# Moving k's transposes into the scores' bank, one factor from VectorE to GpSimd, and two PSUM pools swapped, in a hybrid attention and mLSTM decoder step

## The chip, the cores and the metric

The kernel runs on one core of one Trainium2 chip. The metric is device time in microseconds (us) of that core. PE is the matmul engine (TensorE), DVE is VectorE, ACT is ScalarE, POOL is GpSimd and SP is SyncE, which here only issues DMAs. Each engine takes its own instructions in a fixed order; semaphores hold one back until another engine has done its part.

## The reference, cut to what matters

One decoder layer for 1024 prompt tokens and 8 sample tokens. The change touches the chunkwise mLSTM, the attention of the samples and the gated feed-forward:

```python
h = rmsnorm(x, g_attn_norm); z = h @ w_in
q_a, k_a, v_a, q_m, k_m, v_m, o_m, i_pre, f_pre, gate_a, gate_m = jnp.split(z, in_split_points(), axis=-1)
...
def step(carry, inp):                       # mLSTM, one chunk of tokens
    c, n, m = carry
    ...
    w = d * jnp.einsum('bhtd,bhsd->bhts', qc, kc)
    num = inter[..., None] * jnp.einsum('bhvd,bhtd->bhtv', c, qc) + jnp.einsum('bhts,bhsv->bhtv', w, vc)
    ...
    w_s = jnp.exp(a + b[..., -1:] - m_end[..., None])
    c_new = decay[..., None, None] * c + jnp.einsum('bhs,bhsv,bhsd->bhvd', w_s, vc, kc)
...
x = x + mixed @ w_out
h2 = rmsnorm(x, g_ffn_norm)
x = x + (jax.nn.silu(h2 @ w_gate) * (h2 @ w_up)) @ w_down
```

## The kernel before, in words

All large products run on PE as three passes of split operands (`hh`, `hl` are the high and low parts of the normalised input, `wh`, `wl` those of a weight slice). The first half of the program walks over 128-wide slices of `w_in`: for each slice three column chunks of 344 are multiplied (`gemm`, L226) and evacuated. Between these matmuls a list of generators (`side`) is stepped at a fixed rate; so mLSTM and attention are laid in small pieces between the matmuls of the slices `k`, `v`, `q` and `o`.

The mLSTM works in 8 rounds of 128 tokens, numbered 0 to 7 here by their chunk `c`. `mlstm_a(c)` puts on PE: the scores of the four heads into two banks, `ms_0` and `ms_1` (L559, pool `pa`, each using only the first 256 of a bank's 512 columns); four transposes of v into `mvt` (L563, pool `pt`); two transposes of k into `mkt` (L567, pool `pt`). DVE then multiplies the decay matrix `bmb` by the scores, first those of `ms_0`, then those of `ms_1`, and multiplies the transposed k by a column of weights (`kq` from `mkt`). ACT copies `mvt` to `va`. `mlstm_b` of the round before follows on PE (`my`), then `mlstm_u` (`mu`, which reads `kq`) and `mlstm_d` (transposes into `mh`, pool `pt`, copied by ACT to `hm`). Pool `pt` has two banks, `pa` and `pg` three each; a tile of a pool must wait until the tile that had its bank before has been read.

`mlstm_sample` runs among the rounds; from round 4 to round 6 it gives DVE eight operations on 128x1024 elements (`st`, `scc`, `snum`). `attn_sample` runs among the steps of the prompt's attention. Each `yield` in such a generator ends one piece of it.

What sets the order: PE, SP and POOL keep the order in which the code is written, and so does what is issued through `main_line` on DVE and ACT. The rest of DVE and ACT is placed by a list scheduler, so an edit can reorder them.

After the first part come the gate products (`GateVisit`, tiles `ag`, `bg`, `cg`, `dg`) and, later, the feed-forward (`UpVisit`, `af`, `bf`, `cf`, `df`). Both use a pool `pd` of three tiles of two banks each, laid over the six banks that `pg` and `pa` had. A visit makes seven products, `SEQ`. The first feed-forward visit is split into two single-set visits, on 258 columns each; the other 21 take 516 columns. After the products of a visit, `after` issues the rest: `s1f` and `s2f` get a factor `R`, then a Silu on ACT (L1625), then `R` again (`scale` inside `gate`).

Of the kernel before, what the change touches and what calls it, by code (L numbers as in the profile page):

```python
# [15 lines left out]
ALU = mybir.AluOpType  # L16
# [68 lines left out]
def decoder_step(ctx, tc, x_prompt, x_sample, cache_k, cache_v, st_c, st_n, st_m, rel_bias, w_in, b_if, sinks,  # L85
# [13 lines left out]
    sq = ctx.enter_context(tc.tile_pool(name="sq", bufs=2))  # L99
    pt = ctx.enter_context(tc.tile_pool(name="pt", bufs=2, space=PSUM))  # L100
    banks = ExitStack()
    pg = banks.enter_context(tc.tile_pool(name="pg", bufs=3, space=PSUM))
    pa = banks.enter_context(tc.tile_pool(name="pa", bufs=3, space=PSUM))
    dp = ctx.enter_context(tc.tile_pool(name="dp", bufs=1, space=DRAM))

    def U(name, dt=F32, shape=None):
# [14 lines left out]
    def ps_t(name):  # L121
        return pt.tile([P, 512], F32, tag="t", name=name)
# [426 lines left out]
    def mlstm_a(c, st):  # L549
        bmb, kq, col = st  # L550
        t0 = slice(c * P, (c + 1) * P)
        va = T(f"va{c}", [P, 4, P + 1])
        dve.memset(va[:, :, P:P + 1], 1.0)
        bm2 = bmb.rearrange("p (j u) t -> p u j t", u=2)
        for u in range(2):
            o = 64 * u
            sps = ps_a(f"ms{c}_{u}")
            for j in range(2):
                pe.matmul(sps[:, j * P:(j + 1) * P], mk[j][o:o + 64, t0], mq[j][o:o + 64, t0], start=True, stop=True)  # L559
            tt(dve, bm2[:, u], bm2[:, u], sps[:, 0:256].rearrange("p (j t) -> p j t", t=P), ALU.mult)  # L560
        vps = ps_t(f"mvt{c}")
        for hd in range(4):
            pe.transpose(vps[:, hd * P:(hd + 1) * P], mv[hd][:, t0], ident)  # L563
        act.copy(va[:, :, 0:P], vps.rearrange("p (h v) -> p h v", v=P))
        kps = ps_t(f"mkt{c}")
        for j in range(2):
            pe.transpose(kps[:, j * P:(j + 1) * P], mk[j][:, t0], ident)  # L567
        kw = kq[:, 0:2, :].rearrange("p a (b d) -> p (a b) d", d=64)
        tt(dve, kw, kps[:, 0:256].rearrange("p (h d) -> p h d", d=64), col[:, 1, :].unsqueeze(2).to_broadcast([P, 4, 64]), ALU.mult)
        return bmb, va, kq, kw, col  # L570

    def mlstm_b(c, st):
# [354 lines left out]
    def attn_sample():  # L927
        sc = slice(NP, NT)
        ks = U("ks", shape=[P, NS, P])
        vs = U("vs", shape=[P, NS, P])  # L930
        sp.dma_start(ks, cache_k[0].rearrange("b j k d -> j b (k d)"))
        sp.dma_start(vs, cache_v[0].rearrange("b j k d -> j b (k d)"))
        ps = ps_t("snew")
        pe.transpose(ps[0:NS, 0:P], kT[:, sc], ident)
        pe.transpose(ps[0:NS, P:2 * P], vT[:, sc], ident)
        new = T("snewt", [NS, 2 * P])
        act.copy(new, ps[0:NS, 0:2 * P])
        pool.dma_start(ks[0:1, :, :], new[:, 0:P])
        pool.dma_start(vs[0:1, :, :], new[:, P:2 * P])
        for dst, src, o in ((s_kw, cache_k, 0), (s_vw, cache_v, P)):  # L940
            pool.dma_start(dst[0, :, 0:P - 1], src[0, :, 1:P])
            pool.dma_start(dst[0, :, P - 1].rearrange("b k d -> b (k d)"), new[:, o:o + P])
        for _ in range(AS[0]):
            yield
        kst = U("kst", shape=[P, NS, P])
        for g in range(2):
            ps = ps_t(f"kst{g}")
            for j in range(4):
                pe.transpose(ps[:, j * P:(j + 1) * P], ks[:, 4 * g + j, :], ident)
            act.copy(kst[:, 4 * g:4 * g + 4, :], ps.rearrange("p (b d) -> p b d", d=P))  # L950
        for _ in range(AS[1]):
            yield
        qb = S("qb", [P, NS, 8], 1)
        pool.memset(qb, 0.0)
        for i in range(4):
            pool.tensor_copy(qb[0:64, :, i], qT[i][0:64, sc])
            pool.tensor_copy(qb[64:128, :, 4 + i], qT[i][64:128, sc])
        for _ in range(AS[2]):
            yield
        ps = ps_t("ssT")  # L960
        for b in range(NS):
            pe.matmul(ps[:, 8 * b:8 * b + 8], kst[:, b, :], qb[:, b, :], start=True, stop=True)
        sT = S("sT", [P, 64], 1)
        act.copy(sT, ps[:, 0:64])
        for _ in range(AS[3]):
            yield
        ps = ps_t("ss")
        pe.transpose(ps[0:64, 0:P], sT, ident)
        pr = S("spr", [64, P], 1)
        c = S("sc4", [64, 4], 1)  # L970
        dve.tensor_tensor_reduce(out=pr, in0=ps[0:64, 0:P], in1=bias_s, scale=1.0, scalar=NEG, op0=ALU.add, op1=ALU.max,
                                 accum_out=c[:, 0:1])
        tt(dve, c[:, 0:1], c[:, 0:1], sinks_s, ALU.max)
        tt(dve, c[:, 2:3], sinks_s, c[:, 0:1], ALU.subtract)
        dve.tensor_scalar(c[:, 0:1], c[:, 0:1], -1.0, None, op0=ALU.mult)
        act.activation(pr, pr, AF.Exp, bias=c[:, 0:1], accum_out=c[:, 1:2])
        act.activation(c[:, 2:3], c[:, 2:3], AF.Exp)
        tt(dve, c[:, 1:2], c[:, 1:2], c[:, 2:3], ALU.add)
        dve.reciprocal(out=c[:, 1:2], in_=c[:, 1:2])
        dve.tensor_scalar(pr, pr, c[:, 1:2], None, op0=ALU.mult)  # L980
        for _ in range(AS[4]):
            yield
        ps = ps_t("spt")
        pe.transpose(ps[:, 0:64], pr, ident[0:64, 0:64])
        pT = S("spT", [P, 64], 1)
        act.copy(pT, ps[:, 0:64])
        for _ in range(AS[5]):
            yield
        ps = ps_t("spv")
        for b in range(NS):  # L990
            pe.matmul(ps[:, 8 * b:8 * b + 8], vs[:, b, :], pT[:, 8 * b:8 * b + 8], start=True, stop=True)
        pv = ps[:, 0:64].rearrange("p (b h) -> p h b", h=8)
        for i in range(4):
            dve.tensor_copy(yat[i][0:64, sc], pv[0:64, i, :])
            dve.tensor_copy(yat[i][64:128, sc], pv[64:128, 4 + i, :])
# [601 lines left out]
    class UpVisit(Visit):  # L1597
# [16 lines left out]
        def after(self, n, sets):  # L1614

            box, now, later = self.box, [], []
            s0, s1 = sets[0], sets[-1] + 1
            get = lambda b: self.view(box[b], sets)
            eng = dve if len(sets) == 1 else pool

            def scale(s, th):
                tt(eng, s, s, R["r"][:, th, s0:s1], ALU.mult)

            def gate(s, th):
                act.activation(s, s, AF.Silu)  # L1625
                scale(s, th)
            if n == 0:
                box["p1"] = self.small("p1", sets)
                now.append(lambda: act.copy(box["p1"], get("a")))
            elif n == 2:  # L1630
                box["s1"] = self.small("s1", sets)
                (later if sets == (0,) else now).extend([lambda: tt(dve, box["s1"], get("b"), box["p1"], ALU.add),
                                                         lambda: scale(box["s1"], 0)])
                later.append(lambda: gate(box["s1"], 0))
            elif n == 1:
                box["U2"] = self.small("U2", sets)
                now.append(lambda: act.copy(box["U2"], get("a")))
            elif n == 3:
                box["V"] = self.small("V", sets)
                now.append(lambda: act.copy(box["V"], get("a")))  # L1640

                def c22():
                    if "uu" not in box:
                        box["uu"] = U(f"uu{self.m}", shape=[P, 2, 2, HB])
                    tt(dve, box["uu"][:, 1, s0:s1], get("d"), box["V"], ALU.add)
                later.append(c22)
            elif n == 5:
                box["s2"] = self.small("s2", sets)
                if self.apart(sets):
                    now.append(lambda: tt(dve, box["s2"], get("c"), box["V"], ALU.add))  # L1650
                    now.append(lambda: scale(box["s2"], 1))
                else:
                    now.append(lambda: tt(dve, box["s2"], get("a"), R["r"][:, 1, s0:s1], ALU.mult))
                later.append(lambda: gate(box["s2"], 1))
            elif n == 6:
                u1 = box["uu"][:, 0, s0:s1]
                now.append(lambda: tt(dve, u1, get("d"), box["U2"], ALU.add))
                later.append(lambda: tt(dve, u1, u1, box["s1"], ALU.mult))
                later.append(lambda: tt(dve, box["uu"][:, 1, s0:s1], box["uu"][:, 1, s0:s1], box["s2"], ALU.mult))
            return now, later  # L1660
# [607 lines left out]
```

## Time and profile before

| | |
|---|---|
| time, median of 3 runs | 1391.66 us (1391.24 to 1391.66) |
| the profiled execution: its time, its span | 1391.65 us, 1389.9 us |
| PE busy | 1369.4 us (99%) |
| DVE, ACT, POOL busy | 975.4 us (70%), 617.0 us (44%), 242.0 us (17%) |
| mean granted TensorE clock | 0.997 |

The span is the time from the first to the last instruction in the trace; the 1.75 us beside it lie before and after. Matmuls overlap in the pipeline, so two of them that follow each other without a wait start 0.1 to 0.2 us apart though each is shown with 0.3 us. A square bracket at the end of a row of the timeline gives the idle time of that engine ahead of the row and what ended it.

### The profile page before, as it was taken

Reading aid. Unit: us, or ns where it says so; the run is one execution under the profiler, and the core shown is the slowest. Engines: PE = TensorE matmul, PEld = TensorE weight load, DVE = VectorE, ACT = ScalarE, POOL = GpSimd, SP = SyncE. Lnnn points to the kernel's source line nnn. Section 1 sums busy time; section 2 is a strip of 40 time slices with the busy share of each in tenths; the row PEclk is TensorE's granted clock in tenths of the full one; section 3 lists DMA queues with packets and bytes.
Section 4 is the critical chain, followed back from the end, with each engine's and each line's share of the span. In section 5 each row is a group of like instructions: output and inputs, shape, how many; then the busy total and the mean of one; then the engine's idle time right before and its main releaser. Section 6 shows DMA issues by size and latency. Waiting matters only on the chain.

```text
span 1389.9 us, 26966 instructions
## 1 busy us (share of the span) xinstructions
PE 1369.4 (99%) x10723; PEld 1337.9 (96%) x10724; DVE 975.4 (70%) x1853; ACT 617.0 (44%) x1407; POOL 242.0 (17%) x303
## 2 busy tenths in 40 slices
PE   9999999999999999999999999999999999999996
PEld 7999889999999999999999999999999999999996
DVE  7252758886944444755587888898888878888875
ACT  6243567654443331374454343444433343333325
POOL 4012111001111100001132232333333220000003
PEclk9999999999999999999999999999999999999998
DMA  7144224114233274788423344544434468677633
GB/s 224 32 117 113 62 63 100 31 62 149 81 107 100 84 283 137 221 281 283 166 77 120 110 153 153 168 168 139 131 114 144 146 214 304 220 239 237 221 123 122
DMA packets 179173, 208.42 MB, mean 150 GB/s; under 512 B 20638, under 2 KB 137634, under 8 KB 179032
## 3 DMA queue, kind: packets, MB, share of 16 engines
q1 hardware_dynamic: 161928, 151.72, 35.1%
q0 software_dynamic: 16688, 54.40, 10.7%
q8 instruction: 84, 1.38, 0.4%
q10 hardware_dynamic: 432, 0.59, 0.1%
q14 instruction: 41, 0.34, 0.1%
HBM read 140.31 MB, written 68.96 MB: 151 GB/s over the span
## 4 chain that ended last, share of the span: by engine, by line
PE 90%; DVE 3%; ACT 2%; DMA 2%; issue 1%; POOL 0%; SPq 0%; ACTq 0%; POOLq 0%; DVEq 0%
PE af L1589 18%; PE df L1589 9%; PE ad L1589 7%; PE wo L1261 6%; PE bf L1589 5%; PE ag L1589 4%; PE dd L1589 4%; PE o L226 3%; PE mv L226 3%; PE wm L1385 3%; PE wa L1385 3%; PE q L226 3%; PE dg L1589 2%; PE bd L1589 2%; PE mk L226 2%; PE gm L226 2%
## 5 line engine op out<-in xcount | busy, mean ns | idle before, releaser
L125 POOL TENSOR_TENSOR s1f<-s1f,R 128x516 f32<-128x516 f32 x42 | 68.8, 1637 | 87.2 <-DVE s1f L125 71.5
L1589 PE MATMUL df<-Th,op6f 128*128 128x258 f32 x352 | 67.3, 283 | 1.3 <-DVE uu L125 1.3
L1589 PE MATMUL af<-Th,op0f 128*128 128x258 f32 x352 | 67.4, 284 | 0.0
L1589 PE MATMUL bf<-Th,op2f 128*128 128x258 f32 x352 | 67.3, 283 | 0.0
L1589 PE MATMUL df<-Th,op4f 128*128 128x258 f32 x352 | 67.3, 284 | 0.0
L1589 PE MATMUL af<-Th,op1f 128*128 128x258 f32 x352 | 67.1, 283 | 0.0
L1589 PE MATMUL af<-Th,op3f 128*128 128x258 f32 x352 | 66.9, 283 | 0.0
L1589 PE MATMUL af<-Th,op5f 128*128 128x258 f32 x336 | 64.1, 283 | 0.0
L1625 ACT ACTIVATE s1f<-s1f 128x516 f32<-128x516 f32 (+1 forms) x23 | 14.2, 618 | 103.5 <-POOL s1f L125 103.5
L1589 PEld LDWEIGHTS df<-Th,op6f 128*128 128x128 f32 x352 | 55.9, 189 | 1.5 <-DVE uu L125 1.5
L1589 PEld LDWEIGHTS af<-Th,op1f 128*128 128x128 f32 x352 | 56.0, 189 | 0.0
L1589 PEld LDWEIGHTS af<-Th,op0f 128*128 128x128 f32 x352 | 56.0, 189 | 0.0
L1589 PEld LDWEIGHTS bf<-Th,op2f 128*128 128x128 f32 x352 | 56.0, 189 | 0.0
L1589 PEld LDWEIGHTS df<-Th,op4f 128*128 128x128 f32 x352 | 55.8, 189 | 0.0
L1589 PEld LDWEIGHTS af<-Th,op3f 128*128 128x128 f32 x352 | 55.6, 189 | 0.0
L1589 PEld LDWEIGHTS af<-Th,op5f 128*128 128x128 f32 x336 | 53.4, 190 | 0.0
L125 POOL TENSOR_TENSOR s2f<-s2f,R 128x516 f32<-128x516 f32 x21 | 27.4, 1307 | 135.5 <-ACT s2f L1625 135.4
L1589 PE MATMUL bf<-Tl,op2f 128*128 128x258 f32 x176 | 49.8, 283 | 0.0
L1589 PE MATMUL df<-Tl,op6f 128*128 128x258 f32 x176 | 49.7, 282 | 0.0
L1589 PE MATMUL af<-Tl,op1f 128*128 128x258 f32 x176 | 49.7, 282 | 0.0
L1589 PE MATMUL af<-Tl,op0f 128*128 128x258 f32 x176 | 49.7, 282 | 0.0
L1589 PE MATMUL df<-Tl,op4f 128*128 128x258 f32 x176 | 49.7, 282 | 0.0
(690 smaller groups left out, 4935.9 us busy)
## 6 DMA issues: line engine op xcount, KB each, us to landing
ta<-d_t SPq DMA_DIRECT2D x63, 516.0 KB, 6.6
Yd<-in_w_down_dram SPq DMA_DIRECT2D x40, 256.0 KB, 3.5
d_t<-h POOLq DMA_DIRECT2D x18, 516.0 KB, 5.2
d_t<-t POOLq DMA_DIRECT2D x18, 516.0 KB, 4.6
Xf<-in_w_gate_dram SPq DMA_DIRECT2D x22, 256.0 KB, 4.1
Xf<-in_w_up_dram SPq DMA_DIRECT2D x22, 256.0 KB, 6.9
Yf<-in_w_gate_dram SPq DMA_DIRECT2D x22, 256.0 KB, 3.0
Yf<-in_w_up_dram SPq DMA_DIRECT2D x22, 256.0 KB
```

The costliest lines, as they stand in the source:

```text
L125: return eng.tensor_tensor(out=out, in0=a, in1=b, op=op)
L226: pe.matmul(o, a[:, k, :], b[:, cs], start=(k == 0 and i == 0), stop=(k == n - 1 and i == len(passes) - 1))
L1261: pe.matmul(ps[:, th, 0:HB], a[:, k, :], b, start=(k == 0 and i == 0), stop=(k == KD - 1 and i == 2))
L1385: pe.matmul(ps[:, c, 0:CW], a[:, k, :], b[:, cs], start=(k == 0 and q == 0), stop=(k == 3 and q == 2))
L1589: pe.matmul(ps[:, s if ps.shape[1] > 1 else 0, 0:HB], a, b, start=(first and k == 0 and i == 0), stop=(k == self.nk - 1 and i == 2), skip_ ...
L1625: act.activation(s, s, AF.Silu)
```

## The change

Four edits. The k transposes go to columns 256 to 511 of the round's `ms_1`, in place of an own tile of `pt`. In the single-set visits the factor behind the Silu is issued on POOL in place of DVE; the factor ahead of the Silu stays where it was. `pa` is opened ahead of `pg`, so the two have each other's banks. The samples' attention gets one more `yield`, between its first and second group of key transposes, by which all its later pieces are one step later.

```diff
+    pa = banks.enter_context(tc.tile_pool(name="pa", bufs=3, space=PSUM))
     pg = banks.enter_context(tc.tile_pool(name="pg", bufs=3, space=PSUM))
-    pa = banks.enter_context(tc.tile_pool(name="pa", bufs=3, space=PSUM))
...
-        kps = ps_t(f"mkt{c}")
+        kps = sps[:, 256:512]
         for j in range(2):
             pe.transpose(kps[:, j * P:(j + 1) * P], mk[j][:, t0], ident)
...
-        tt(dve, kw, kps[:, 0:256].rearrange("p (h d) -> p h d", d=64), col[:, 1, :].unsqueeze(2).to_broadcast([P, 4, 64]), ALU.mult)
+        tt(dve, kw, kps.rearrange("p (h d) -> p h d", d=64), col[:, 1, :].unsqueeze(2).to_broadcast([P, 4, 64]), ALU.mult)
...
             act.copy(kst[:, 4 * g:4 * g + 4, :], ps.rearrange("p (b d) -> p b d", d=P))
+            if g == 0:
+                yield
...
-            def scale(s, th):
-                tt(eng, s, s, R["r"][:, th, s0:s1], ALU.mult)
+            def scale(s, th, on=None):
+                tt(on or eng, s, s, R["r"][:, th, s0:s1], ALU.mult)

             def gate(s, th):
                 act.activation(s, s, AF.Silu)
-                scale(s, th)
+                scale(s, th, pool)
```

On PE, in round 4 of the mLSTM, before: the last scores, the transposes of v (`mvt`) and of k (`mkt`), and the next matmuls of the slice `v`.

```order
L559 MATMUL ms_1_1730<-mq_139,mk_141 128x128
L563 MATMUL mvt_1734<-cst,mv_142 128x128
L563 MATMUL mvt_1734<-cst,mv_143 128x128
L563 MATMUL mvt_1734<-cst,mv_144 128x128
L563 MATMUL mvt_1734<-cst,mv_145 128x128
L567 MATMUL mkt_1740<-cst,mk_140 128x128 [waits Activation_49]
L567 MATMUL mkt_1740<-cst,mk_141 128x128
L226 MATMUL v_1720<-hh_124,wl_v 128x344
```

The same place on PE with the change.

```order
L559 MATMUL ms_1_1726<-mq_139,mk_141 128x128
L563 MATMUL mvt_1730<-cst,mv_142 128x128
L563 MATMUL mvt_1730<-cst,mv_143 128x128
L563 MATMUL mvt_1730<-cst,mv_144 128x128
L563 MATMUL mvt_1730<-cst,mv_145 128x128
L567 MATMUL ms_1_1726<-cst,mk_140 128x128 [waits DVE_49]
L567 MATMUL ms_1_1726<-cst,mk_141 128x128
L226 MATMUL v_1716<-hh_124,wl_v 128x344
```

The order of PE is the same. The k transposes wait for DVE where they waited for an ACT copy; the count that they wait for is the one that DVE gives when it has multiplied `bmb` by the same round's `ms_1`. It is so in all 8 rounds, while `mkt` before waited in rounds 1 to 3 for the `kq` multiply of the round before and in rounds 4 to 7 for ACT's copies of an earlier `mh`.

On DVE, in rounds 4 and 5, before: `st`, `scc` and `snum` are the wide steps of the samples' state, `wl_q` the low part of a weight slice, `num` the scaling of an earlier round's output.

```order
L619 TENSOR_SCALAR num_1632<-num_1632,mrd 128x128 x4
L125 TENSOR_TENSOR st_1416<-sv,sk 128x1024
L125 TENSOR_TENSOR bmb_1598<-bmb_1598,ms_0_1726 128x2x128
L125 TENSOR_TENSOR bmb_1598<-bmb_1598,ms_1_1730 128x2x128
...
L125 TENSOR_TENSOR st_1416<-scc_1415,sq 128x1024
L125 TENSOR_TENSOR bmb_1711<-bmb_1711,ms_0_1864 128x2x128
L125 TENSOR_TENSOR bmb_1711<-bmb_1711,ms_1_1868 128x2x128
L125 TENSOR_TENSOR mrd<-mrd,msq 128x4
L708 TENSOR_REDUCE snum<-st_1416 128x16
```

The same place on DVE with the change.

```order
L125 TENSOR_TENSOR st_1415<-sv,sk 128x1024
L615 TENSOR_SCALAR msq<-msq 128x4
L716 RECIPROCAL sden<-sden 128x1
L704 SCALAR_TENSOR_TENSOR scc<-scc,swe,st_1415 128x1024
L125 TENSOR_TENSOR bmb_1595<-bmb_1595,ms_0_1722 128x2x128
L125 TENSOR_TENSOR bmb_1595<-bmb_1595,ms_1_1726 128x2x128
...
L615 TENSOR_SCALAR msq<-msq 128x4
L708 TENSOR_REDUCE snum<-st_1415 128x16
L125 TENSOR_TENSOR bmb_1707<-bmb_1707,ms_0_1859 128x2x128
L125 TENSOR_TENSOR bmb_1707<-bmb_1707,ms_1_1863 128x2x128
```

Round 4's multiplies have moved ahead of `num` and behind `scc`; round 5's have moved behind the second `snum`, which also stands ahead of them now.

On POOL, at the first feed-forward visits, with the change: `d_x` are DMAs of the residual, `rrs` the rows' norm.

```order
L1340 DMA d_x_7_199<-x_111_7085 128x258
L125 TENSOR_TENSOR s1f_0_8186<-s1f_0_8186,R 128x258
L125 TENSOR_TENSOR rrs_7663<-rrs_7663,nhalf_200 128x3
L125 TENSOR_TENSOR s2f_0_8280<-s2f_0_8280,R 128x258
L125 TENSOR_TENSOR s1f_1_8336<-s1f_1_8336,R 128x258
L125 TENSOR_TENSOR s2f_1_8449<-s2f_1_8449,R 128x258
L125 TENSOR_TENSOR s1f_0_8495<-s1f_0_8495,R 128x516 x2
```

Four multiplies of 258 columns have come to POOL, the first of them ahead of the power of `rrs`; before, `rrs` followed the DMAs and was followed by the rows of 516 columns.

## The prediction

> **What bounds the kernel now.** I read the page first, then PE's table of waits, then the timelines of PE, DVE and ACT at the three places that the edits touch. The page's first row says that PE is the bound. The waits of PE say how little there is to win.
>
> ```profile
> PE 1369.4 (99%) x10723; PEld 1337.9 (96%) x10724; DVE 975.4 (70%) x1853; ACT 617.0 (44%) x1407; POOL 242.0 (17%) x303
> ...
> PE mkt L567 <- ACT hm L631: 2.0, 2, 1.1
> ...
> PE df L1589 <- DVE uu L125: 1.3, 1, 1.3
> ...
> PE ag L1589 <- ACT sg L1084: 0.6, 1, 0.6
> ...
> PE at L885 <- ACT kst L950: 0.4, 1, 0.4
> ...
> PE mu L595 <- DVE bmb L125: 0.3, 1, 0.3
> ```
>
> PE keeps its order and never has work to pull forward, so a microsecond for which it stands still in the middle is a microsecond of the time, and the reverse. The table names each edit's target: 2.0 us for `mkt`, 1.3 us for `df`, 0.6 us for `ag`, 0.4 us for `at`. All four together are 4.3 us of 1391.65. A measurement of this kernel can tell about 0.2% (2.8 us) from no change.
>
> **Edit 1, the k transposes.** What it removes: `mkt` no longer needs a bank of `pt`, so the two waits for `hm` go (2.0 us: 1.10 in round 5, 0.88 in round 7, in the rows below). What it adds is in the order of the changed program: in each of the 8 rounds the k transposes now wait for DVE's multiply of `bmb` by the same round's `ms_1`, since that multiply reads the tile they write. Behind them in PE's queue stands everything else, the slices' matmuls first. So the question is how far behind L567 on PE that multiply ends. The rows of L567, rounds 0 to 7, behind the first row of `mvt`:
>
> ```profile
> 126.85 0.66 PE L563 MATMUL mvt<-cst,mv 128*128 128x128 f32 x4
> 127.34 0.38 PE L567 MATMUL mkt<-cst,mk 128*128 128x128 f32 x2
> ...
> 131.18 0.38 PE L567 MATMUL mkt<-cst,mk 128*128 128x128 f32 x2
> ...
> 138.10 0.38 PE L567 MATMUL mkt<-cst,mk 128*128 128x128 f32 x2
> ...
> 146.82 0.38 PE L567 MATMUL mkt<-cst,mk 128*128 128x128 f32 x2
> ...
> 156.93 0.38 PE L567 MATMUL mkt<-cst,mk 128*128 128x128 f32 x2
> ...
> 167.83 0.44 PE L567 MATMUL mkt<-cst,mk 128*128 128x128 f32 x2 [1.10 <-ACT hm L631]
> ...
> 178.34 0.38 PE L567 MATMUL mkt<-cst,mk 128*128 128x128 f32 x2
> ...
> 188.75 0.44 PE L567 MATMUL mkt<-cst,mk 128*128 128x128 f32 x2 [0.88 <-ACT hm L631]
> ```
>
> And DVE's multiplies by the scores (x2 is `ms_0` and `ms_1`; in rounds 0 and 7 they are rows of their own, and this is the one by `ms_1`):
>
> ```profile
> 127.54 0.42 DVE L125 TENSOR_TENSOR bmb<-bmb,ms 128x256 f32<-128x256 f32 x1
> ...
> 130.84 0.75 DVE L125 TENSOR_TENSOR bmb<-bmb,ms 128x256 f32<-128x256 f32 x2 [2.54 <-issue]
> ...
> 138.75 0.75 DVE L125 TENSOR_TENSOR bmb<-bmb,ms 128x256 f32<-128x256 f32 x2
> ...
> 147.85 0.75 DVE L125 TENSOR_TENSOR bmb<-bmb,ms 128x256 f32<-128x256 f32 x2
> ...
> 160.43 0.75 DVE L125 TENSOR_TENSOR bmb<-bmb,ms 128x256 f32<-128x256 f32 x2
> ...
> 172.10 0.75 DVE L125 TENSOR_TENSOR bmb<-bmb,ms 128x256 f32<-128x256 f32 x2
> ...
> 180.45 0.75 DVE L125 TENSOR_TENSOR bmb<-bmb,ms 128x256 f32<-128x256 f32 x2 [0.56 <-ACT bmb L543]
> ...
> 190.81 0.42 DVE L125 TENSOR_TENSOR bmb<-bmb,ms 128x256 f32<-128x256 f32 x1
> ```
>
> In none of the rounds has the multiply ended when L567 starts. Start plus duration, less the start of L567 (less its bracket in rounds 5 and 7), gives the lags 0.62, 0.41, 1.40, 1.78, 4.25, 6.12, 2.86 and 3.36 us; to each I add 0.05 us until PE goes on, an estimate from the gap between a released row and the end of its releaser in these timelines.
>
> Rounds 0 to 3 I take as they are: what DVE does ahead of the multiply hangs on PE's `my` of the round before, which moves with PE, and the order of DVE there is unchanged. That is 0.67 + 0.46 + 1.45 + 1.83 = 4.41 us. From round 4 on the lag is DVE's own backlog, the wide steps of the samples' state, and PE's delay eats it. Round 4: PE comes 4.41 us later against a lag of 4.25 us, so only the shortest lag is left, round 1's, where DVE stood idle before the scores: 0.46. Round 5: PE arrives at 166.73 + 4.87 = 171.60. The multiply must follow ACT's exponentials of this round, and ACT, in the changed order, does four `hm` copies, half a split, an evacuation, four squares and the four exponentials in a row once PE's `mh` has ended:
>
> ```profile
> 162.99 0.60 PE L629 MATMUL mh<-cst,num 128*128 128x128 f32 x4
> ...
> 167.03 0.74 ACT L631 COPY hm<-mh 128x128 f32<-128x128 f32 x4
> ...
> 169.06 0.40 ACT L614 ACTIVATE mj<-num,mrd 128x128 bf16<-128x128 f32 x1
> ...
> 169.59 0.40 ACT L614 ACTIVATE mj<-num,mrd 128x128 bf16<-128x128 f32 x1
> ...
> 170.28 1.28 ACT L543 ACTIVATE bmb<-bmb,cols 128x128 f32<-128x128 f32 x4 [0.20 <-DVE bmb L125]
> ```
>
> From 167.03 to 171.56 that is 4.53 us, less the 0.20 us idle, plus one square more (0.53 from start to start): 4.86. `mh` ends at 163.59 + 4.87 = 168.46, ACT at 168.5 + 4.9 = 173.4, and the pair of multiplies (0.75) at 174.2: PE waits 2.65. DVE's own work from round 4's multiply to this one, 172.85 - 161.18 = 11.67 us before, with `num` added and a few small steps gone, ends at about the same time (173.9). Round 6: the multiply stands behind the scaling of an earlier `num`, whose chain starts at PE's `my`; ACT has the exponentials and the `hm` copies (1.28 + 0.74) in it where round 3 had a split (1.14).
>
> ```profile
> 139.27 1.05 PE L579 MATMUL my<-va,bmb 128*128 128x129 f32 x8
> ...
> 142.75 1.14 ACT L231 ACTIVATE wh_q<-ws_q 128x512 fp32r<-128x512 f32 x2
> ...
> 169.04 1.05 PE L579 MATMUL my<-va,bmb 128*128 128x129 f32 x8
> ```
>
> Round 3's chain took 148.60 - 139.27 = 9.33 us; plus 0.88 it is 10.21. Both starts below are less the 1.10 us gone and plus 7.52 us of waits so far: `my` at 175.46, the multiply done at 185.67, and L567, also less `mu`'s 0.30, at 184.46: 1.26 with the 0.05. Round 7's multiply keeps its place behind a weight split that waits for ACT; its lag lies between the floor of 0.46 and round 6's 1.26, and I take the middle, 0.86, having no row that is nearer. The sum of the new waits: 4.41 + 0.46 + 2.65 + 1.26 + 0.86 = **9.64 us**. Bounds: the floor in all rounds, 8 x 0.46 = 3.7; no backlog eaten, 20.8 + 0.4 = 21.2. The waits that go: 1.98 and, as `kq` is ready long before, 0.30. **Edit 1: +7.4 us.**
>
> **Edit 2, the factor on POOL.** In the first single-set visit DVE stands still for the Silu; some 4 us later `df` waits for its `uu` (the 1.3 us of the table). The first row is that visit's, the others are from the first visit of 516 columns.
>
> ```profile
> 703.82 0.43 DVE L125 TENSOR_TENSOR s1f<-s1f,R 128x258 f32<-128x258 f32 x1 [1.53 <-ACT s1f L1625]
> ...
> 727.57 0.68 DVE L125 TENSOR_TENSOR op5f<-S4f,op5f 128x512 fp32r<-128x512 f32 x1
> ...
> 727.79 1.62 POOL L125 TENSOR_TENSOR s1f<-s1f,R 128x516 f32<-128x516 f32 x1 [19.25 <-DVE s1f L125]
> ...
> 728.17 1.79 DVE L125 TENSOR_TENSOR op6f<-Yf,op6f 128x512 fp32r<-128x512 f32 x1
> ```
>
> Without it DVE is 1.53 + 0.43 = 1.96 us earlier, against 1.3 us to win. A POOL multiply on 258 columns is shown nowhere; between nothing and the 1.62 us of 516 columns I take half, 0.8, as the width is half. It isn't free for DVE: the row at 728.17 takes 1.79 us beside POOL's, where the like row ahead of it takes 0.68, so 1.1 us are lost per 1.6 us of POOL, 0.5 per multiply here. DVE keeps 1.4 us of lead. **-1.3 us**, and nothing if POOL takes the lead away. POOL's power of `rrs` now stands behind the first multiply, which the bound of nothing won covers. [...]
>
> **Edit 3, the pools.** The first `ag` no longer needs the bank of the last `sg`, so its 0.6 us go. But the third product writes the same bank once ACT has copied `p1g`, and that copy is late on its own account:
>
> ```profile
> 378.04 0.35 ACT L1692 COPY p1g<-ag 128x258 f32<-128x258 f32 x1
> ...
> 378.45 0.38 PE L1589 MATMUL ag<-gh,op1g 128*128 128x258 f32 x1
> ```
>
> It ends at 378.39 and `ag` follows 0.06 later; started 0.59 earlier, PE would wait here instead. **0.0**, between -0.6 and 0.
>
> **Edit 4, the yield.** The 0.4 us for `kst` go. In the changed order `ss` and `spv` stand directly behind eight transposes in the same two banks, so each waits for ACT's copy of the first four.
>
> ```profile
> 131.38 0.59 ACT L564 COPY va<-mvt 128x512 f32<-128x512 f32 x1 [1.56 <-PE mvt L563]
> ```
>
> Such a copy takes 0.59 us while the second four take 0.49 (126.85 to 127.34 above): 0.1 us at least, 0.6 if ACT is busy; 0.35 each. **+0.3**, between -0.4 and +0.8.
>
> **Sum:** 9.64 - 2.28 - 1.3 + 0.0 + 0.3 = +6.4 us on the profiled execution's 1391.65 us, which is the median of the runs within 0.01: **1398.0 us.**
>
> **The rivals.**
> - *Shallow waits.* If rounds 4 to 7 all shrink to the floor, the new waits are 4.41 + 1.84 = 6.25 and the time is 1394.6. For it: PE's delay grows. Against: rounds 5 to 7 hang on chains that start at PE's own `my` and `mh`.
> - *Deep waits.* If half of the old lags of rounds 4 to 7 stays, halfway between my 5.23 and their 16.8, the waits are 15.4 and the time is 1403.8. DVE's changed order, with one wide step more ahead of round 5's multiply, speaks for it.
> - *Faster.* If DVE had multiplied by `ms_1` before the four `mvt` transposes (0.49 us) are through, the wait would cost nothing and only the gains stand: -2.28 - 1.3 - 0.4, 1387.7. It decides at a multiply that ends 0.41 us earlier than in the quickest round shown; no row speaks for it.
> - *The clock falls.* The mLSTM rounds ran at full clock, the end of the program, where PE is busy for 18.70 of 30 us, at 0.85 (the third number from the right):
>
> ```profile
> 120.00:205.00 85.00, 82.72 (x635) 74.11 (x634) 50.03 (x173) 49.40 (x177) 16.07 (x21) 1.00 0.29 76
> ...
> 1360.00:1390.00 30.00, 18.70 (x155) 17.51 (x154) 15.64 (x46) 17.44 (x45) 13.78 (x16) 0.85 0.36 141
> ```
>
>  At 0.85 for 30 us it would cost 4.5 us more: 1402.5. Against it, PE would still be busy for 82.72 of 85 + 7.4 us of this stretch, 90%. [...]
> - *POOL gives nothing.* If edit 2's 1.3 us stay, 1399.3.
>
> **How the numbers follow.** Forecast 0.60, shallow 0.12, deep 0.12, faster 0.04, clock 0.05, POOL 0.07. The range 1394.6 to 1402.5 leaves out the faster case, the deep one and some of the shallow one's lower part. Slower by over 0.2% is above 1394.4: all but the faster case and about two thirds of the shallow one, 0.88; within 0.2%: 0.08; faster: 0.04.
>
> **What would show it.** Right: PE's waits list L567 waiting for DVE `bmb` 8 times, some 8 to 11 us in total with the longest in round 5; no `mkt` or `df` wait; an `ag` wait for `p1g`. Wrong: L567 waits of under 4 us, or of over 15, in total; a granted clock under 1.00 in the rounds; a longer stall of PE at a place that I gave nothing.

## The result, and the profile after

The changed kernel takes **1404.32 us** (median of 4 runs, 1403.26 to 1405.45) against 1391.45 of the kernel before in the same job: ratio **1.0092, 95% interval 1.0077 to 1.0107**, 12.9 us slower. Forecast were 1398.0 us and a range of 1394.6 to 1402.5. The sign was right and the size was half. The profiled execution took 1403.26 us, 11.6 more than the profiled 1391.65; the account below is of these two.

The page's first row and PE's waits in the changed kernel (waits: total, times, longest):

```profile
PE 1373.1 (98%) x10723; PEld 1340.6 (96%) x10724; DVE 974.9 (70%) x1849; ACT 617.6 (44%) x1407; POOL 246.1 (18%) x307
```

```profile
PE ms L567 <- DVE bmb L125: 11.0, 8, 2.6
...
PE ag L1591 <- ACT p1g L1694: 0.9, 1, 0.9
...
PE xr L1204 <- ACT x L1201: 0.5, 1, 0.5
PE ag L1591 <- ACT U2g L1700: 0.4, 1, 0.4
PE ss L970 <- ACT apt L889: 0.2, 1, 0.2
PE spv L993 <- ACT apt L889: 0.2, 1, 0.2
```

`mkt`, `df`, `mu` and `at` are gone. In their place stands L567, eight times, waiting for DVE's `bmb`. The same by stretches of time, the third number from the right being the granted clock:

```profile
120.00:205.00 85.00, 74.04 (x537) 65.28 (x536) 45.73 (x151) 41.84 (x141) 14.17 (x19) 0.96 0.30 76
175.00:180.00 5.00, 4.20 (x22) 4.00 (x24) 2.11 (x11) 0.79 (x3) 0.11 (x1) 0.66 0.72 205
...
190.00:195.00 5.00, 5.00 (x28) 4.76 (x29) 0.94 (x4) 0.61 (x2) 0.00 (x0) 0.68 0.00 0
```

PE is busy for 74.04 us of this stretch, before for 82.72, and the clock was below 1.00 twice. The trace's clock records have it at 0.50 from 176.09 us and from 189.74 us, each time for 3.413 us. PE's timeline shows what stands ahead of both. L567 of rounds 0 to 7, and two of the `my`:

```profile
128.06 0.44 PE L567 MATMUL ms<-cst,mk 128*128 128x128 f32 x2 [0.50 <-DVE bmb L125]
...
132.40 0.44 PE L567 MATMUL ms<-cst,mk 128*128 128x128 f32 x2 [0.30 <-DVE bmb L125]
...
140.84 0.44 PE L567 MATMUL ms<-cst,mk 128*128 128x128 f32 x2 [1.29 <-DVE bmb L125]
...
151.44 0.44 PE L567 MATMUL ms<-cst,mk 128*128 128x128 f32 x2 [1.66 <-DVE bmb L125]
...
163.33 0.44 PE L567 MATMUL ms<-cst,mk 128*128 128x128 f32 x2 [1.57 <-DVE bmb L125]
...
164.55 1.05 PE L579 MATMUL my<-va,bmb 128*128 128x129 f32 x8
...
175.80 0.45 PE L567 MATMUL ms<-cst,mk 128*128 128x128 f32 x2 [2.62 <-DVE bmb L125]
...
177.76 1.90 PE L579 MATMUL my<-va,bmb 128*128 128x129 f32 x8
...
189.98 0.69 PE L567 MATMUL ms<-cst,mk 128*128 128x128 f32 x2 [2.28 <-DVE bmb L125]
...
201.75 0.44 PE L567 MATMUL ms<-cst,mk 128*128 128x128 f32 x2 [0.73 <-DVE bmb L125]
```

A bracket shows a little less than the delay, since the row ahead is still shown as busy for 0.17 us when L567 could have started. Counted as the forecast counts it (from the start of `mvt` plus 0.49), the delays are 0.67, 0.47, 1.47, 1.83, 1.74, 2.79, 2.45 and 0.89: 12.31 us. The `my` behind round 5's wait takes 1.90 instead of 1.05: it ran at the half clock.

Apart from the pieces of the samples' attention that edit 4 moves, PE's instructions stand in the same order in both kernels, so the starts of one and the same instruction can be subtracted. Round 7's L567 starts at 201.75, before at 188.75: **+13.0 us** by the end of the rounds. Of it 12.31 are waits, -2.28 the waits that went, and the remaining 2.97 go to the two stretches at half clock, in which the difference is seen to grow by 1.59 us (7.97 to 9.56) and 1.52 us (11.64 to 13.16). Behind the samples' attention the difference is 13.1 (`kst` gone, `ss` and `spv` come); at the first `ag` it falls by 0.86 and 4 us later rises by 0.84, and at `df` it falls by 1.58. 13.0 + 0.1 + 0.0 - 1.58 = 11.5 of the 11.6 us.

### The profile page after: what moved, and what is told of

It is laid out like the page before. It is cut to its first block, busy times and chain, and to the rows that moved or that the text cites. A ratio compares the mean times of both kernels' runs of the same rounds, so it can differ in the third digit from the quotient of the medians.

```text
span 1401.4 us, 26965 instructions
## 1 busy us (share of the span) xinstructions
PE 1373.1 (98%) x10723; PEld 1340.6 (96%) x10724; DVE 974.9 (70%) x1849; ACT 617.6 (44%) x1407; POOL 246.1 (18%) x307
## 3 DMA queue, kind: packets, MB, share of 16 engines
q0 software_dynamic: 16688, 54.40, 10.5%
## 4 chain that ended last, share of the span: by engine, by line
PE 91%; DVE 3%; ACT 2%; DMA 1%; issue 1%; POOL 0%; SPq 0%; POOLq 0%; ACTq 0%; DVEq 0%
PE af L1591 18%; PE df L1591 9%; PE ad L1591 7%; PE wo L1263 6%; PE bf L1591 5%; PE ag L1591 4%; PE dd L1591 4%; PE o L226 3%; PE mv L226 3%; PE wm L1387 3%; PE wa L1387 3%; PE q L226 3%; PE dg L1591 2%; PE bd L1591 2%; PE mk L226 2%; PE gm L226 2%
## 5 line engine op out<-in xcount | busy, mean ns | idle before, releaser
L125 POOL TENSOR_TENSOR s1f<-s1f,R 128x516 f32<-128x516 f32 (+1 forms) x44 | 70.8, 1610 | 77.4 <-DVE s1f L125 55.3
L1627 ACT ACTIVATE s1f<-s1f 128x516 f32<-128x516 f32 (+1 forms) x23 | 14.2, 618 | 104.2 <-POOL s1f L125 104.2
L125 POOL TENSOR_TENSOR s2f<-s2f,R 128x516 f32<-128x516 f32 (+1 forms) x23 | 29.3, 1274 | 144.3 <-ACT s2f L1627 138.8
```

Source lines behind the costliest of these rows:

```text
L125: return eng.tensor_tensor(out=out, in0=a, in1=b, op=op)
```

## The experiments

Two theories stood at the start. *Waits and clock*: all of the loss is L567's place behind DVE's multiply, by the waits and by a clock that falls behind the longest of them. *Rivals*: part of it comes from the swapped pools, the yield or POOL; or from sharing a bank as such; or rounds 4 and 6 are deep for another reason than the order on DVE.

**Edit 1 alone, and all but edit 1.**

```diff
 e1_only (before, and)
-        kps = ps_t(f"mkt{c}")
+        kps = sps[:, 256:512]
...
 no_e1 (after, and)
-        kps = sps[:, 256:512]
+        kps = ps_t(f"mkt{c}")
...
```

> The kernel before with edit 1 alone (k's transposes into the second half of ms_1). Theory: the whole loss is edit 1. The trace of the changed kernel shows 12.3 us by which L567 goes on late in the 8 rounds and two stretches of 3.41 us at half clock, 3.4 us; the waits for mkt (2.0) and mu (0.3) are gone. 12.3 + 3.4 - 2.3 = +13.4 on 1391.5: about 1404.9, a little above the changed kernel, since edit 2's gain of 1.3 is not in it. PE should wait 8 times at L567 for DVE's bmb, about 11 us by the table, the longest in round 5. Rival: part of the loss is an interaction with the swapped pools or the extra yield; then edit 1 alone costs clearly less than the changed kernel, about 1401 (waits less gains, +9.6) or lower.

> The changed kernel without edit 1 (edits 2, 3 and 4 alone, k's transposes in their own bank again). Theory: edits 2 to 4 are worth -1.45 (the df wait) + 0.3 (ag) + 0.0 (kst against ss and spv), so 1390.3; PE waits for mkt about 2.0 again, none at L567 for DVE, the clock stays at full speed until the end. Rival: the three others carry part of the loss, through the pools or through POOL's longer multiplies; then it is over 1392.

Edit 1 alone: ratio **1.0102 (1.0088 to 1.0116)**, 14.2 us. Without it: **0.9990 (0.9981 to 0.9998)**, 1.4 us faster. Together that is 12.8 of the 12.9 us of the whole, and no interaction is needed. Edit 1 alone, the stretch of the rounds:

```profile
120.00:205.00 85.00, 73.88 (x522) 65.42 (x521) 44.79 (x145) 41.67 (x139) 13.90 (x19) 0.94 0.33 73
```

PE's busy time is the changed kernel's within 0.2 us, but the clock is 0.94 and not 0.96: three falls of 3.413 us instead of two, behind rounds 4, 5 and 6. Round 4's wait is deeper here, its bracket 2.19 us instead of 1.57; round 6's, with a fall behind it too, is 1.79 instead of 2.28.

**Transposes between the scores, and ahead of them.** Both kernels put k's transposes into the free half of `ms_1` and let nothing be written there once DVE reads.

```diff
 k_first (before, transposes removed behind mvt, and)
+            if u == 1:
+                kps = sps[:, 256:512]
+                for j in range(2):
+                    pe.transpose(kps[:, j * P:(j + 1) * P], mk[j][:, t0], ident)
             for j in range(2):
                 pe.matmul(sps[:, j * P:(j + 1) * P], ...
 k_ahead (before, transposes removed behind mvt, and)
+        mss = [ps_a(f"ms{c}_{u}") for u in range(2)]
+        kps = mss[1][:, 256:512]
+        for j in range(2):
+            pe.transpose(kps[:, j * P:(j + 1) * P], mk[j][:, t0], ident)
         for u in range(2):
             o = 64 * u
-            sps = ps_a(f"ms{c}_{u}")
+            sps = mss[u]
```

> The kernel before with k's transposes in the second half of ms_1, but issued ahead of that bank's two score matmuls, so that nothing is written into the bank after DVE has begun to read it. Theory: what costs is only the place in the order, behind a read of the same tile; here L561 waits for nothing new, the mkt wait (2.0) and mu's go, the scores come some 0.2 us later in each round without anyone waiting for that: 1391.5 - 2.3 = 1389.2, full clock in the rounds. Rival: sharing the bank costs by itself, since DVE's reading of k's half now holds a bank of pa until later, so that my, mu or the next scores wait for it: 1392 to 1400, with new waits for DVE kq at those lines.

> The kernel before with k's transposes in the second half of ms_1, issued ahead of the scores of both banks. In k_first, where they stood between the scores of ms_0 and of ms_1, no wait was added and yet each round took 0.77 us more (round 0: from the first score to the next slice's matmul 1.29 before, 2.06 there): the four matmuls of each bank then took 0.71 where all eight took 0.72. Theory: the scores use 64 rows each, and those of the two banks run beside each other on the two halves of the array; the transposes, on all 128 rows, stood between them. Ahead of both they break nothing up: the mkt waits (2.0) and mu's (0.3) are gone and nothing new comes, ratio 0.9983, 2.3 us less than before. Rival: it is the sharing of the bank between transposes and scores that costs 0.77 per round; then this is like k_first, 2.5 to 3.7 us over before.

`k_first` missed: **1.0017 (1.0008 to 1.0026)**, 2.4 us slower, and no wait to show for it. Its rows of round 0 on PE, and behind them those of `k_ahead`:

```profile
126.18 0.71 PE L563 MATMUL ms<-mq,mk 64*128 64x128 f32 x4
126.82 0.44 PE L561 MATMUL ms<-cst,mk 128*128 128x128 f32 x2
127.18 0.71 PE L563 MATMUL ms<-mq,mk 64*128 64x128 f32 x4
127.82 0.66 PE L567 MATMUL mvt<-cst,mv 128*128 128x128 f32 x4
```

```profile
126.33 0.38 PE L558 MATMUL ms<-cst,mk 128*128 128x128 f32 x2
126.64 0.72 PE L563 MATMUL ms<-mq,mk 64*128 64x128 f32 x8
127.29 0.66 PE L567 MATMUL mvt<-cst,mv 128*128 128x128 f32 x4
```

Four score rows take the 0.64 us (126.18 to 126.82) in which eight go when nothing stands between them (126.64 to 127.29). The scores of `ms_0` read partitions 0 to 63 of q and k and those of `ms_1` partitions 64 to 127, and with nothing between them the two banks took together the time of one; with the two transposes between them each bank took its own 0.64 us (the second from 127.18 to 127.82). Ahead of both, `k_ahead` is **0.9986 (0.9977 to 0.9996)**, 2.0 us faster than before. It has small waits of its own in its table: 0.5 us at `mvt`, 0.2 at `mh`, and 0.9 at `mu` where there were 0.3. So neither the shared bank nor the transposes cost anything that the time shows, only their place.

**The order on DVE.** The two multiplies are issued through `main_line`, which keeps them in the order of the code; so far the list scheduler placed them.

```diff
-            tt(dve, bm2[:, u], bm2[:, u], sps[:, 0:256]...
+            main_line(tt, dve, bm2[:, u], bm2[:, u], sps[:, 0:256]...
```

> The changed kernel with DVE's two multiplies of bmb by the scores kept in the order of the code, so that the scheduler no longer puts scc (round 4) and round 7's bmb addition with msq and the scaling of num (round 6) ahead of them. Theory: the depth of rounds 4 and 6 is DVE's order and nothing else: round 4's wait falls from 1.6 to about 0.5, round 6's from 2.3 to about 0.5, round 5's stays near 2 (ACT's exponentials end it); the total delay at L567 falls from 12.3 to about 8, no stretch at half clock behind rounds 4 and 6, and the time is 1404.3 - 4.3 - 1.7 to 3.4: 1397 to 1398.5. Rival: the late load of bmb, which hangs on PE, and ACT's exponentials behind it end those waits too: rounds 4 and 6 keep over 1.5 us, and the time stays above 1402.

L567 of rounds 4 to 7:

```profile
164.11 0.44 PE L567 MATMUL ms<-cst,mk 128*128 128x128 f32 x2 [0.74 <-DVE bmb L125]
...
175.88 0.69 PE L567 MATMUL ms<-cst,mk 128*128 128x128 f32 x2 [1.93 <-DVE bmb L125]
...
188.91 0.44 PE L567 MATMUL ms<-cst,mk 128*128 128x128 f32 x2 [1.14 <-DVE bmb L125]
...
199.25 0.44 PE L567 MATMUL ms<-cst,mk 128*128 128x128 f32 x2 [0.73 <-DVE bmb L125]
```

The brackets of rounds 4 and 6 are halved (1.57 to 0.74, 2.28 to 1.14) and L567's total in the table of waits is 8.1 instead of 11.0, the way of the theory, though it had about 0.5 in both. The time missed the 1397 to 1398.5 us expected: **1.0079 (1.0065 to 1.0093)**, 1404.03 us, an interval that overlaps the changed kernel's. In the profiled execution the rounds end 10.5 us late instead of 13.0. A fall moved to behind round 3 (1.66 us), so there were two again.

**Filling the waits.** Matmuls on zeros into `mvt`'s bank, ahead of v's transposes.

```diff
         vps = ps_t(f"mvt{c}")
+        for _ in range({4: 5, 5: 9, 6: 12}.get(c, 0)):      # fill_5: 9 in round 5 alone
+            pe.matmul(vps, wz[:, 0:P], wz, start=True, stop=True)
```

> The changed kernel with nine matmuls of 512 columns on zeros in round 5 alone, written into mvt's bank ahead of v's transposes; they compute nothing that is used. They fill about 1.9 us (estimate, from 344 columns in some 0.14 us) of the 2.6 us for which PE stood still there. Theory: the clock fell because of that wait, and round 6 waits 2.3 instead of 1.2 us because its chain ran at half clock. Then the clock stays full in round 5 (-1.7), round 6's wait falls to about 1.2 (-1.1) and its own fall of the clock goes too (-1.7): 1404.3 - 4.5 = 1399.8. Rival 1: round 6 is deep for reasons of its own (the order on DVE): only -1.7, 1402.6, and a stretch at half clock behind round 6. Rival 2: the clock falls by the load over a longer time, whatever the one wait: no change, 1404.3.

> The changed kernel with 5, 9 and 12 matmuls of 512 columns on zeros ahead of v's transposes in rounds 4, 5 and 6, which compute nothing that is used (some 1.05, 1.9 and 2.5 us). So far the clock fell for one window of 3.413 us behind each window in which PE stood still for 1.67 us or more, at no place with 1.42 or less, and with 1.56 to 1.67 it did both. Theory: with the fills no window has over 1.5 us idle, the clock stays full in the rounds, and the runs agree within 0.6 us. Of the price: behind round 5 a fall is mostly absorbed by round 6's wait (round 5's end to round 6's: 14.2 us with a fall, 13.7 without), behind round 6 it costs its 1.7 us in full, so 1404.3 - 0.5 - 1.7 = 1402.1, or 1401.1 against the profiled 1403.3. Rival: each fall costs its 1.7 us: 1400.9 or less. Other rival: the clock falls by something else and the runs still spread over 2 us.

Both missed: **1.0077 (1.0064 to 1.0091)** and **1.0094 (1.0080 to 1.0108)**. The filling of round 5 is shown with 1.89 us in both, as estimated, though matmuls of 344 columns start 0.15 to 0.16 us apart in the traces, not 0.14. In `fill_5` no fall came behind round 5, but one came behind round 4 (1.56 us), and round 6's wait grew to 3.40 us. In `fill_4_5_6` DVE's order was another one: a scaling of `num`, which waits for POOL, now stood ahead of round 5's multiply, and 2.35 us remained there behind the filling. So these two don't isolate the clock; they show that round 6's depth doesn't need a fall behind round 5. One fall in `fill_4_5_6`, at 317.6 us, lies far behind the rounds. The window ahead of it holds 0.24 us idle and the 16 matmuls of `spv`, on 8 columns each, from 315.10 to 316.91 us: 2.05 us together. In the eleven other traces no window holds more than 1.81 us of `spv` and the idle time around it, and nothing fell there. What made the clock fall at this place was not tried by itself.

**The fall of the clock by itself.**

```diff
+    def stall(count):
+        t = ps_t("stall")
+        pe.transpose(t[:, 0:P], ident, ident)
+        for _ in range(count):
+            main_line(act.copy, warm, t[:, 0:1])
+        pe.transpose(t[:, 0:P], ident, ident)
...
+                    if n == 2 and s == 1 and k == 2 and 4 <= getattr(self, "m", 0) < 20:
+                        stall(4 + self.m)
```

> The kernel before with one stall of PE in the middle of the bf product of each of 16 feed-forward visits, where PE is otherwise never idle: a transpose into a free bank, 8 to 23 copies of one column from it by ACT, which is idle there (one copy more from visit to visit), and a second transpose into the bank, which waits for them. By some 0.13 us a copy (estimate, from ACT's 128x32 and 128x4 rows in the mLSTM rounds, 0.11 to 0.13 apart) the stalls run from about 1.3 to 3.3 us. This measures the fall of the clock by itself. Theory: a stall that leaves some 1.6 us or more idle within one 3.413 us window halves the clock for the next window, and that visit is 1.7 us longer than its stall makes it; below 1.4 us nothing falls; in between, and up to twice that, it depends on how the window's edge cuts the stall. So 5 to 12 of the 16 fall, the shortest never. Rival: it takes idleness of nearly a whole window; then only the longest stalls fall, 2 or fewer. Other rival: the falls in the mLSTM rounds came from the small matmuls and waits around, not from the stall; then none falls here. Time: 1392 plus the stalls (16 x 2.3 = 37 us) plus 1.7 a fall, about 1430 to 1450.

1467.55 us, ratio 1.0543 (1.0527 to 1.0559), above the 1430 to 1450 expected; the stalls were longer than estimated, 1.59 to 4.45 us, 48.7 in all. Ten of the 16 made the clock fall. Two neighbours, cut into windows of 3.413 us along the grid on which this run's falls lie, to within 0.05 us (the second row of each pair of stretches begins where the first ends; the clock is the third number from the right):

```profile
828.87:832.28 3.41, 2.27 (x19) 2.03 (x18) 2.75 (x4) 0.89 (x6) 1.01 (x1) 1.00 0.02 5
832.28:835.69 3.41, 2.52 (x21) 2.53 (x22) 1.43 (x3) 1.84 (x7) 0.58 (x1) 1.00 0.01 2
852.77:856.18 3.41, 1.25 (x11) 1.02 (x10) 2.86 (x3) 2.04 (x12) 1.09 (x1) 1.00 0.89 359
856.18:859.60 3.42, 3.42 (x18) 3.42 (x18) 2.05 (x3) 0.76 (x2) 1.28 (x1) 0.51 0.02 8
```

The first stall is 2.02 us long, the second 2.16. The first is cut by a window's edge into 1.19 and 0.83 us, and nothing falls. The second lies within one window, PE is busy for 1.25 of 3.41 us, and the next window runs at half clock with 18 matmuls. Over all 16, every window at full clock with 1.90 us or more idle was followed by a fall and none with 1.78 or less: a stall of 3.17 us, cut into 1.78 and 1.39, passed. From the end of a stall to the next it takes 20.60 to 20.68 us without a fall, 21.82 to 22.16 with one, 23.01 to 23.18 where a second window followed at half clock: **about 1.35 us a fall** in the mean, 1.5 where the whole slow window lies behind the stall and less where the stall reaches into it. A second slow window followed where the first still had 1.00 us or more idle (five times), and not at 0.66 or less. In the rounds it fell at a little less, and at no one number: falls behind 1.56 (`fill_5`, round 4), 1.66 (`mul_main`, round 3) and 1.67 us (`e1_only`, round 6), none behind 1.62 (`no_e1`) and 1.66 (round 3 of the changed kernel).

**The best version.**

```diff
 k_ahead_e2 = k_ahead and edit 2; k_ahead_all = after, k's transposes as in k_ahead
```

> k_ahead and edit 2 (the factor behind the Silu on POOL). If k_ahead's theory holds and edit 2 is worth the 1.3 us of the df wait, this is 3.6 us under before, ratio 0.9974, and below both kernels. Rival: POOL's longer multiplies hold DVE up later and edit 2 is worth nothing: equal to k_ahead.

> The changed kernel (all four edits) with k's transposes issued ahead of the scores of both banks in place of behind v's. Theory: edits 3 and 4 are worth nothing together, so this equals k_ahead with edit 2, ratio 0.9977 to the kernel before (1389 us); the whole loss of the changed kernel, 12.9 us, was the place of two transposes. Rival: the swapped pools or the later pieces of the samples' attention cost by themselves (no_e1 was 0.4 us short of edit 2's 1.7 in k_ahead_e2 against k_ahead): ratio 0.9985 or above.

**0.9977 (0.9968 to 0.9986)**, 1389.09 us, and **0.9979 (0.9970 to 0.9989)**, 1389.13 us: both are below both kernels, and edits 3 and 4 add nothing that can be measured. `k_ahead_all`, the stretch of the rounds:

```profile
120.00:205.00 85.00, 84.11 (x644) 75.55 (x642) 49.32 (x173) 49.61 (x179) 16.08 (x21) 1.00 0.30 76
```

With the same four edits, but the two transposes of each round ahead of its scores, PE is busy for 84.11 us instead of 74.04, at full clock.

## Why the prediction was right and wrong

**Edit 1, rounds 0 to 3, 5 and 7: right, round 7 by luck.** Forecast 0.67, 0.46, 1.45, 1.83, 2.65, 0.86; measured 0.67, 0.47, 1.47, 1.83, 2.79, 0.89. A lag read from the trace before holds where what stands ahead of it moves with the waiting engine or ends a chain from it. In round 5 the two chains of the forecast do end together: ACT's last exponential at 174.92 us, the wide `snum` on DVE at 175.08, just as the multiply starts (175.00). Round 7's multiply kept its place behind the weight split, but its 0.86 was the middle between the floor and round 6's 1.26, and that bound was 2.45.

**Edit 1, round 4: mis-sized, 0.46 against 1.74.** The step that failed is "PE's delay eats it", the backlog of DVE. Round 4's addition on DVE before, the issue of its load by SP before and after, and DVE after:

```profile
153.43 0.69 DVE L125 TENSOR_TENSOR bmb<-bmb,cst 128x512 f32<-128x512 f32 x1 [2.45 <-DMA bmb<-d_bm]
```

```profile
146.17 0.74 SPq L529 DMA_DIRECT2D bmb<-d_bm  x1
```

```profile
148.96 0.72 SPq L529 DMA_DIRECT2D bmb<-d_bm  x1
```

```profile
155.92 0.69 DVE L125 TENSOR_TENSOR bmb<-bmb,cst 128x512 f32<-128x512 f32 x1 [3.56 <-DMA bmb<-d_bm]
...
161.34 1.27 DVE L704 SCALAR_TENSOR_TENSOR scc<-scc,swe,st 128x1024 f32<-128x1024 f32 x1
162.53 0.74 DVE L125 TENSOR_TENSOR bmb<-bmb,ms 128x256 f32<-128x256 f32 x2
...
186.54 0.69 DVE L125 TENSOR_TENSOR bmb<-bmb,cst 128x512 f32<-128x512 f32 x1 [1.34 <-DMA bmb<-d_bm]
187.15 0.16 DVE L615 TENSOR_SCALAR msq<-msq 128x4 f32<-128x4 f32 x1
188.50 0.16 DVE L125 TENSOR_TENSOR mrd<-mrd,msq 128x4 f32<-128x4 f32 x1 [1.18 <-POOL msq L125]
...
188.79 0.48 DVE L619 TENSOR_SCALAR num<-num,mrd 128x128 f32<-128x128 f32 x2
189.18 0.74 DVE L125 TENSOR_TENSOR bmb<-bmb,ms 128x256 f32<-128x256 f32 x2
```

The backlog was no fixed block of work. It begins with an addition that waits for a load, and SP issued that load 2.79 us later (146.17 to 148.96). SP issues it right behind two loads of a weight slice (`ws_q`), which wait for DVE's split `wl_q`; and that split (143.75 before, 146.54 with the change) stands directly behind a step of DVE that waits for PE's `mu`. So the load came late by about what PE was late after round 2, 2.74 us. The addition came 2.49 us later, the multiply 2.10 (160.43 to 162.53), and PE's transposes 4.67 (156.93 to 161.60 without their wait): of the old lag, 4.25 and the 0.05, about 1.73 us stayed. `e1_only` shows the same from another side: there the addition came 0.38 us later still (156.30) and the wait was 0.62 deeper (2.19). Besides, the scheduler put `scc` (1.27 us) ahead of the multiply, where it followed it before. In `mul_main`, where the scaling of `num` stands ahead of the multiply in place of `scc`, 0.83 us of the wait went; how the 1.28 us divide between the load and `scc` was not tried with one of them alone.

**Edit 1, round 6: mis-sized, 1.26 against 2.45.** The rows from 186.54 on show the chain: round 7's addition, waiting for its DMA, stands ahead of `msq`; `msq` goes to POOL and back (1.18 us); the scaling of `num` and then the multiply follow. The forecast built the chain from round 3's and had the scaling in it, but not that DMA ahead of `msq`. `mul_main` has the multiply ahead of that addition, and 1.14 us of the bracket went.

**The clock: a rival at 0.05 that came true, 2.97 us.** It was priced at 4.5 us (0.85 for 30 us) and rejected because PE would still be busy for 90% of the stretch. An average over 85 us was the wrong view: in `stalls` the clock fell behind every window of 3.413 us with 1.90 us or more idle, and round 5's 2.62 us lie in one such window, 77% of it. The falls of a run lie on one grid of 3.413 us: the two of the changed kernel start 13.65 us apart, four steps. Where the grid lies against the program differs: in `e1_only` the first fall starts at about 164.1 us, half a step off the changed kernel's grid (estimate, from its clock of 0.91 between 160 and 165 us).

Together: 7.4 + 1.28 + 1.19 + 0.20 (the other rounds) + 2.97 = 13.0. *Deep waits* came near the time (1403.8) by another way: it had 15.4 us of waits, and there were 12.3 and the clock.

**Edit 2: right**, -1.3 forecast, -1.58 measured at `df`, and 1.25 us between `k_ahead_e2` and `k_ahead` by their ratios, whose intervals overlap. POOL after, and on DVE a split alone and one beside POOL's multiply:

```profile
717.09 1.30 POOL L125 TENSOR_TENSOR s1f<-s1f,R 128x258 f32<-128x258 f32 x1 [1.64 <-ACT s1f L1627]
718.35 1.87 POOL L125 TENSOR_TENSOR rrs<-rrs,nhalf 128x3 f32<-128x3 f32 x1
```

```profile
715.41 1.22 DVE L125 TENSOR_TENSOR Tl<-xg,Th 128x1032 fp32r<-128x1032 f32 x1
...
717.83 1.65 DVE L125 TENSOR_TENSOR Tl<-t,Th 128x1032 fp32r<-128x1032 f32 x1
```

The first multiply took 1.30 us, not 0.8 (the other three 1.22, 0.79 and 0.64), and DVE's split 1.65 instead of 1.22: 0.4 us lost where 0.5 was allowed for.

**Edit 3: right, 0.0.** The `ag` wait turned from `sg` (0.6) to `p1g` (0.9) as told; what PE gained there, 0.86 us, it gave back within 4 us. **Edit 4: right**, +0.3 forecast, +0.1 measured; `ss` and `spv` wait 0.2 each.

What stays open: the timed runs of the changed kernel lie up to 2 us above the profiled one. One more fall would explain about 1.4 of it. It would lower the mean clock of a run by 0.001; the two longest runs have 0.994 against the profiled 0.995, which fits, but the run of 1403.39 us has 0.992, which does not. No trace of those runs is kept.

## What to carry to other kernels

When two tiles share a bank, look at the order in which they are written: what went in ahead of the first reader's release cost nothing here (`k_ahead`, 2.0 us faster than before), what went in behind it waited for the reader, 12.31 us in eight rounds. Price a new wait on the matmul engine per window of 3.413 us, not per stage: in `stalls` 1.90 us or more idle in one window cost another 1.35 us behind it, so by these numbers two waits of 1.5 us would be cheaper than one of 2.5; no run tried that. And before counting on a delay to eat a backlog on another engine, ask whether any of it starts at a load or a buffer that the delayed engine releases, and whether the scheduler leaves its order: here 1.73 of round 4's 4.30 us stayed. The same holds for an experiment: filling a wait with matmuls changed the order that the list scheduler chose for DVE, and the wait moved instead of being filled.

## What was new about the hardware

- In `stalls` the clock fell to half for one window of 3.413 us (or two) behind every window with 1.90 us or more idle, and behind none with 1.78 or less; in the rounds of other runs it fell behind 1.56, 1.66 and 1.67 us and did not fall behind 1.62 and 1.66. The length of a stall alone didn't decide: 3.17 us cut in two passed, 2.16 us in one window did not.
- Two transposes of 128x128 between score matmuls of 64x128 cost 0.77 us in round 0 of `k_first` (1.29 to 2.06) without any wait in the table: PE was shown as busy all the time.
- One fall, in `fill_4_5_6`, came behind a window with only 0.24 us idle beside 1.81 us of matmuls of 8 columns; it was seen once, and its cause was not tried.
